# A two-layer decoder trunk on one core: seven block products for eight in half of an output projection, with changed orders around it

## The chip, the cores and the metric

The kernel runs on one core of a Trainium2 chip. Its time is the device time of one execution in microseconds. TensorE (PE) multiplies matrices, VectorE (DVE) and ScalarE (ACT) work element by element, GpSimd (POOL) and SyncE (SP) start transfers here. The kernel before has a median of 2151.49 us over three runs (2151.22 to 2151.53).

## The reference, cut to what matters

The trunk has 256 positions of 2048 features in float32. Layer 0 runs two recurrent mixers side by side, RG-LRU on 1024 features and HGRN2 on 1024, joins them and maps them by one output projection; layer 1 is an attention with its own output projection. Each layer ends in a squared-ReLU MLP of width 8192. The change touches the gates of the RG-LRU and the two output projections.

```python
def rg_lru(xb, w_a, b_a, w_i, b_i, lam):
    ...
    r = jax.nn.sigmoid(jnp.einsum('bshi,hij->bshj', xh, w_a.astype(F32)).reshape(bsz, seq, LRU_WIDTH)
                       + b_a.astype(F32))
    i = jax.nn.sigmoid(jnp.einsum('bshi,hij->bshj', xh, w_i.astype(F32)).reshape(bsz, seq, LRU_WIDTH)
                       + b_i.astype(F32))
    log_a = -LRU_C * r * jax.nn.softplus(-lam.astype(F32))
    ...

def recurrent_mixers(h, w_in, conv_w, conv_b, w_a, b_a, w_i, b_i, lam, lower_bound, g_norm, w_out):
    proj = h @ w_in
    x_lru, y_lru, q_h, f_h, v_h, g_h = jnp.split(proj, list(IN_SPLITS), axis=-1)
    lru = rg_lru(causal_depthwise_conv(x_lru, conv_w, conv_b), w_a, b_a, w_i, b_i, lam)
    lru = lru * jax.nn.gelu(y_lru.astype(F32), approximate=True)
    hg = hgrn2(q_h, f_h, v_h, g_h, lower_bound, g_norm)
    mixed = jnp.concatenate([lru, hg], axis=-1).astype(h.dtype)
    return mixed @ w_out
```

The residual is added to the result, and layer 0's MLP follows with its norm. In layer 1 the joined heads of the attention go through `w_o` in the same way.

## The kernel before, in words

**Numbers.** A float32 value is kept as a high and a low part. A product of two such values is three matmuls: high by high, high by low, low by high. Weights arrive as units of 128 x 2048 (1 MB, on SP's queue); ACT casts a unit to its high part (line 116, `hi`) and DVE subtracts to get the low part (line 117, `lo`). `bufa` and `bufb` hold a stage's input features as 16 blocks of 128 features, with the high half at columns 0 to 255 and the low half behind it.

**The order on each engine** is fixed when the program is built: a scheduler places the instructions by priority (`urgent`, `stream`) and by the order in which they are written, and `chain` strings all matmuls of line 210 in the written order. `units` is the written order of all weight units. `unit` hands out the next one and lets `fetch` load the one two places behind it.

**The recurrent stage** walks through units in the order of a string: x units give the conv's inputs, y units the gate branch, h units the heads of HGRN2, g units the gates. `lru_gates(gp)` (line 549) does four blocks of features, each with two gates `gr` and `gi`: a gate is two blocks by three matmuls of 256 columns, with a PSUM tile `p` of its own, and ACT's sigmoid (line 241 by its helper `lut`) reads it. The next weight unit is given to a list `late` there, and its cast is bound to come after the third gate's sigmoid (`gates[3:4]`, through `behind`). Pieces of HGRN2 (`po`, `pl`, `pt`, lines 484 to 527) and the recurrence (`z`, `q`, lines 584 to 588) lie between and beside these matmuls.

**An output projection** (`out_project`) runs over four groups of 512 columns. For one group, `tokens` takes two PSUM tiles, one per half of the rows (`j`), and four weight units `g`, each with four feature blocks. With `by_k`, as in the first group, the loop goes over feature blocks and takes both row halves for each; otherwise it finishes one half first. Layer 0's order of units is `kgs` = (2, 3, 0, 1), so that HGRN2's features, which are units 2 and 3, come first. `add_res` (line 629) adds to the residual, and `to_features` turns the new residual into the MLP's input and, for the first two groups, makes the linear combinations `formx` that the next paragraph needs (lines 612 to 618).

**Seven products for eight.** `blocks` multiplies two halves of the rows by two column groups over half of the feature blocks as a 2 x 2 block product with seven block products instead of eight (a, t1, t2, t3, t4, c, d); the other half of the features is done plainly (`n`). The combinations on the weight side are sums of whole units: `combine` makes them with DVE adds (line 148, `s`) and with loads that add onto a unit in memory on POOL's queue (`t`, `s`). The combinations on the input side are `formx` and `formh`. In before, `first` (over `w1`), `second` (over `w2`) and the q/k/v projection use it. `ORDERS` are the orders of its units; two of them differ in which of the plain units n 6 and n 7 comes first.

**Attention's end** (around line 932): for each head two matmuls into `po`, then ACT's cast into `bufb` (line 268), which layer 1's projection reads.

Of the kernel before, what the change touches and what calls it, by code (L numbers as in the profile page):

```python
# [10 lines left out]
F32 = mybir.dt.float32  # L11
# [4 lines left out]
AF = mybir.ActivationFunctionType  # L16
OP = mybir.AluOpType
# [3 lines left out]
P = 128  # L21
S = 256
D = 2048
KB = D // P
# [17 lines left out]
def trunk_kernel(ctx, tc, head, x, xtok, cols, tab, masks, pos, fin, w_in, w_gate, w_out, w_qkv, w_o, w1, w2, out):  # L42
# [27 lines left out]
    units = []  # L70
# [5 lines left out]

    order_of = lambda src, i: ORDERS[0 if src is w1 else 2 if src is w2 and i == 120 else 1]

# [6 lines left out]
    for step in ORDER.split():  # L85
        src, first, n = where[step[0]]
        units.extend((src, first(int(step[1])) + i) for i in range(n))
    units.extend((w_out, 4 * n + g) for n in range(4) for g in (2, 3, 0, 1))
    for layer in range(2):
# [11 lines left out]
    class Weights:  # L101
        def __init__(self, raw, step=2048, behind=()):
            self.raw = raw
            self.hi = whi.tile([P, 2048], F32R, name="hi")
            self.lo = wlo.tile([P, 2048], F32R, name="lo")
            self.behind = list(behind)
            for at in range(0, 2048, step) if step else ():
                self.split(at, step)

        def split(self, at, n, w=None):  # L110
            h, l = self.part(at, n)
            if w is None:
                w = self.raw[:, at:at + n]
            else:
                h, l = (t.rearrange("p (k c) -> p k c", c=512) for t in (h, l))
            casts[:] = [after(A.copy(h, w), self.behind)]  # L116
            i = V.tensor_tensor(l, w, h.bitcast(F32), OP.subtract)  # L117
            self.ins = getattr(i, "ins", i)
# [3 lines left out]

    def fetch(late=None):
        u = at[0]
        if u >= len(units):
            return
        at[0] += 1
        src, i = units[u][:2]
        with stream():
            if len(units[u]) > 2:  # L130
                combine(u, *units[u])
                return
            r = wraw.tile([P, 2048], F32, name="raw")
            loads[:] = [after(nc.sync.dma_start(r, src[i]), [])]
            if late is not None:
                late.append((u, r))
                return
            made[u] = Weights(r, 1024)
# [59 lines left out]

    def unit(src, i, late=None):
        u = at[1]  # L200
        assert units[u][0] is src and units[u][1] in (None, i), (u, i)
        at[1] += 1
        if u + 2 >= at[0]:
            fetch(late)
        return made.pop(u)
# [3 lines left out]
    def mm(*args, **kw):  # L209
        chain[:] = [after(T.matmul(*args, **kw), chain)]  # L210
# [123 lines left out]

    def tokens(src, i0, mov, kgs=(0, 1, 2, 3), by_k=False):
        ks = range(KB)
        ps = [pmm.tile([P, 512], F32, name="p") for _ in range(2)]
        for g in kgs:
            w = unit(src, i0 + g)
            order = [(j, i) for i in range(4) for j in range(2)] if by_k else \  # L340
                [(j, i) for j in range(2) for i in range(4)]
            for j, i in order:
                k = ks[4 * g + i]
                h, l = w.part(i * 512, 512)
                xh = mov[:, k, j * P:j * P + P]
                xl = mov[:, k, S + j * P:S + j * P + P]
                first, last = g == kgs[0] and i == 0, g == kgs[-1] and i == 3
                mm(ps[j], xh, h, start=first, stop=False)
                mm(ps[j], xh, l, start=False, stop=False)
                mm(ps[j], xl, h, start=False, stop=last)  # L350
            turn_some(1)
        return ps

# [195 lines left out]
    def lru_gates(gp):  # L549
        late, gates = [], []  # L550
        w = unit(w_gate, gp, late)
        gr = wk.tile([P, 4, S], F32, name="gr", bufs=1)
        gi = wk.tile([P, 4, S], F32, name="gi", bufs=1)
        for m in range(4):
            b = 4 * gp + m
            for gate, (g, bname) in enumerate(((gr, "b_a"), (gi, "b_i"))):
                p = pmm.tile([P, 512], F32, name="p")
                direct(p, w, [(gate * 8 + 2 * m + k, bufb[:, (b // 2) * 2 + k], k == 0, k == 1)
                              for k in range(2)])
                with urgent():  # L560
                    lut(g[:, m], p[:, :S], AF.Sigmoid, bias=col(bname, b))
                    gates.append(luts["now"][-1])
        with stream():
            for u, r in late:
                made[u] = Weights(r, 1024, gates[3:4])
        for m in range(4):
# [87 lines left out]

    def out_project(src, gname, kgs):
        nrm = Norm()
        for n in range(4):
            add_res(tokens(src, 4 * n, bufb, kgs, by_k=not n), n, nrm)
            to_features(n, gname, formx if n < 2 else None)
        return nrm  # L660

    nrm = out_project(w_out, "nmlp0", (2, 3, 0, 1))

# [115 lines left out]

    def second(i0, n0, nrm, r2, r2n, done, gains):  # L780
        def to_x(bank, j, n, r, last):
            at = slice(n * 512, n * 512 + 512)
            with urgent():
                read[:] = [after(V.scalar_tensor_tensor(xres[:, j, at], bank, r[:, j:j + 1], xres[:, j, at],
                                                        op0=OP.mult, op1=OP.add), [])]
                if nrm and last:
                    nrm.add(j, n, 0, S if ending and (j, n) == (1, LAST) else 512)
# [19 lines left out]
        def u3(bank):  # L807
            to_x(bank, 1, n0 + 1, r2n, True)
            done(n0 + 1)

        blocks(w2, i0, n0, bufb, formh,
               {"a": lambda b: to_x(b, 0, n0, r2, False), "t1": lambda b: to_x(b, 1, n0 + 1, r2, False),
# [4 lines left out]
    def mlp(layer, nrm, nxt, gname):  # L817
# [35 lines left out]
        return fing  # L853

    nx1 = Norm()
    mlp(0, nrm, nx1, "nmix1")
# [72 lines left out]
    def mix(hd, st, vg, bank="po", bufs=1):  # L929
        vs = slice((hd % 8) * P, (hd % 8) * P + P)  # L930
        po = psc.tile([P, S], F32, name=bank, bufs=bufs)
        T.matmul(po, vg[:, 0, vs], st[:, :S], start=True, stop=False, skip_group_check=True)  # L932
        T.matmul(po[:, P:], vg[:, 1, vs], st[:, S:], start=False, stop=True, skip_group_check=True)
        split_to(bufb[:, hd], po)
# [3 lines left out]

    lastv = []

# [48 lines left out]
    pair, formh = open_pairs(1)  # L989
    nrm = out_project(w_o, "nmlp1", (0, 1, 2, 3))  # L990
    fnorm = Norm(False)
# [82 lines left out]
def _layout(a):  # L1074
# [25 lines left out]
    def gate(w):  # L1100
# [19 lines left out]
        "fin": c(n(a["final_norm"]).reshape(1, D)),  # L1120
        "w_in": c(np.concatenate(w_in)), "w_gate": c(w_gate), "w_out": c(toks(n(a["rec_w_out"][0]))),
        "w_qkv": c(np.concatenate(w_qkv)), "w_o": c(toks(n(a["attn_w_o"][0]))),
# [20 lines left out]
```

## Time and profile before

| | |
|---|---|
| median of three runs | 2151.49 us (2151.22 to 2151.53) |
| profiled execution | 2151.35 us |
| its span | 2149.5 us |
| mean granted TensorE clock | 0.999 |
| data read from HBM | 481.76 MB, 225 GB/s over the span |
| cast of whole raw units on ACT (line 116) | 462 of 1494 ns mean |
| low part of them on DVE (line 117) | 462 of 1771 ns mean |

The profile is one execution, 1.85 us longer in device time than its span from the first to the last instruction. Terms of a sum that are worked out from the trace stand against this execution. A timeline row gives the start, the duration, the engine, the source line, the operation with its output and inputs, and in brackets the idle time before it and what ended that. Durations of matmuls overlap: the distance between starts says what one costs.

### The profile page before, as it was taken

The page shows a single profiled execution, that of the slowest core. Times are in us where ns is not written, and L with a number is a line of the kernel's source. Part 1 is how long each engine was busy: PE and PEld are TensorE (multiplying, and loading weights), DVE is VectorE, ACT ScalarE, POOL GpSimd, SP SyncE. Part 2 cuts the span into 40 slices and gives each one's busy share as a digit, 9 for nine tenths or more (in the row PEclk, how much of TensorE's full clock was granted, in tenths as well). Part 3 has the DMA queues.
Part 4 walks back from the last instruction along what each step waited for, and adds up shares of the span by engine and source line. Part 5 has one row for each costly group of instructions (what it writes and reads, how often), then busy time and mean ns, then how long its engine had stood idle before and what let it go on. Part 6 is the DMA issues. An engine that isn't in the chain of part 4 may idle for free.

```text
span 2149.5 us, 27705 instructions
## 1 busy us (share of the span) xinstructions
PE 2136.2 (99%) x11018; PEld 1830.3 (85%) x11018; DVE 1786.9 (83%) x2087; ACT 1267.6 (59%) x1407; POOL 61.8 (3%) x77
## 2 busy tenths in 40 slices
PE   9999999999999999999999999999999999999998
PEld 8999998888888888888888888888888888888887
DVE  7776787788888888889988897867988988888897
ACT  7444485566466566557665545456655755755764
POOL 0000000000000000000000000000000000000000
PEclk9999999999999999999999999999999999999999
DMA  8544445588878888887785556457878788787885
GB/s 323 175 157 157 154 149 209 179 240 268 249 240 263 257 243 243 277 245 234 240 268 198 173 160 232 157 185 226 237 240 283 240 240 260 262 241 243 272 261 156
DMA packets 68160, 485.64 MB, mean 226 GB/s; under 512 B 7600, under 2 KB 7856, under 8 KB 10048
## 3 DMA queue, kind: packets, MB, share of 16 engines
q1 hardware_dynamic: 57600, 410.89, 52.0%
q0 software_dynamic: 10144, 72.39, 18.3%
q8 instruction: 86, 1.41, 0.3%
q10 hardware_dynamic: 288, 0.61, 0.1%
q14 instruction: 42, 0.34, 0.0%
HBM read 481.76 MB, written 2.10 MB: 225 GB/s over the span
## 4 chain that ended last, share of the span: by engine, by line
PE 96%; ACT 2%; DVE 1%; DMA 0%; issue 0%; SPq 0%
PE p L210 66%; PE pd L210 13%; PE po L210 12%; PE pl L213 2%; PE pl L489 1%; PE pt L210 1%; DVE lo L117 1%; ACT hi L116 1%; DMA both_in<-in_head 0%; PE pl L911 0%; ACT gi L241 0%; ACT L241 0%; PE po L932 0%; PE pd L924 0%; ACT gr L241 0%; DVE xc L577 0%
## 5 line engine op out<-in xcount | busy, mean ns | idle before, releaser
L116 ACT CAST hi<-raw 128x2048 fp32r<-128x2048 f32 (+1 forms) x462 | 679.1, 1494 | 564.2 <-PE p L210 343.0
L117 DVE TENSOR_TENSOR lo<-raw,hi 128x2048 fp32r<-128x2048 f32 (+1 forms) x462 | 810.9, 1771 | 206.2 <-ACT hi L116 190.9
L210 PE MATMUL p<-hi,bufb 128*128 128x512 f32 x1408 | 449.0, 391 | 1.5 <-DVE z L438 1.1
L210 PE MATMUL p<-bufa,hi 128*128 128x256 f32 (+1 forms) x1792 | 367.2, 317 | 0.1
L210 PE MATMUL p<-hi,bufa 128*128 128x512 f32 x1136 | 363.3, 390 | 0.7 <-ACT bufa L271 0.7
L210 PEld LDWEIGHTS p<-hi,bufb 128*128 128x128 f32 x1408 | 264.3, 188 | 56.8 <-DVE z L438 1.5
L210 PEld LDWEIGHTS p<-bufa,hi 128*128 128x128 f32 x1792 | 294.9, 190 | 18.6 <-DVE hz L438 0.3
L210 PE MATMUL p<-lo,bufb 128*128 128x512 f32 x704 | 274.2, 390 | 0.0
L210 PE MATMUL p<-bufa,lo 128*128 128x256 f32 x1152 | 256.2, 287 | 0.0
L210 PEld LDWEIGHTS p<-hi,bufa 128*128 128x128 f32 x1136 | 213.1, 188 | 45.0 <-ACT bufa L271 0.9
L117 DVE TENSOR_TENSOR lo<-s,hi 128x2048 fp32r<-128x2048 f32 x102 | 233.1, 2285 | 14.5 <-ACT hi L116 12.3
L116 ACT CAST hi<-s 128x2048 fp32r<-128x2048 f32 x102 | 195.1, 1913 | 51.7 <-PE po L210 22.2
L210 PE MATMUL p<-lo,bufa 128*128 128x512 f32 x568 | 221.4, 390 | 0.2 <-DVE lo L117 0.2
L210 PEld LDWEIGHTS p<-bufa,lo 128*128 128x128 f32 x1152 | 189.7, 191 | 2.7
L210 PEld LDWEIGHTS p<-lo,bufb 128*128 128x128 f32 x704 | 132.2, 188 | 26.9
L210 PEld LDWEIGHTS p<-lo,bufa 128*128 128x128 f32 x568 | 106.6, 188 | 22.6 <-DVE lo L117 0.6
L210 PE MATMUL pd<-hi,bufa 128*128 128x512 f32 x288 | 95.2, 392 | 0.0
L210 PE MATMUL p<-hi,formx 128*128 128x512 f32 x288 | 94.8, 390 | 0.0
L117 DVE TENSOR_TENSOR lo<-t,hi 128x2048 fp32r<-128x2048 f32 x34 | 77.8, 2288 | 13.0 <-ACT hi L116 13.0
L210 PE MATMUL po<-hi,bufa 128*128 128x512 f32 x256 | 84.9, 393 | 0.0
L210 PE MATMUL p<-hi,formh 128*128 128x512 f32 x256 | 84.0, 389 | 0.0
L210 PE MATMUL pd<-hi,bufb 128*128 128x512 f32 x256 | 83.0, 389 | 0.0
(307 smaller groups left out, 2892.0 us busy)
## 6 DMA issues: line engine op xcount, KB each, us to landing
raw<-in_w SPq DMA_DIRECT2D x224, 1024.0 KB, 6.5
raw<-in_w_qkv SPq DMA_DIRECT2D x46, 1024.0 KB, 4.9
raw<-in_w_in SPq DMA_DIRECT2D x45, 1024.0 KB, 4.9
t<-in_w SPq DMA_DIRECT2D x32, 1024.0 KB, 6.4
t<-in_w POOLq DMA_DIRECT2D x32, 1024.0 KB, 8.9
s<-in_w POOLq DMA_DIRECT2D x32, 1024.0 KB, 9.3
raw<-in_w_out SPq DMA_DIRECT2D x16, 1024.0 KB, 4.9
raw<-in_w_o SPq DMA_DIRECT2D x16, 1024.0 KB, 4.8
```

The source lines that it names most:

```text
L116: casts[:] = [after(A.copy(h, w), self.behind)]
L117: i = V.tensor_tensor(l, w, h.bitcast(F32), OP.subtract)
L210: chain[:] = [after(T.matmul(*args, **kw), chain)]
L213: chain[:] = [after(T.transpose(out_, in_, ident), chain)]
L489: T.matmul(pl[:, j], kq[:, js], halves(qp[:, js], c, True), start=True, stop=True)
```

## The change

Layer 0's output projection does its third and fourth column groups by `second`, that is by `blocks` with seven products for eight over feature blocks 0 to 7, and plainly over 8 to 15. `mixed_forms` makes the combinations of the projection's input out of `bufb` for four pairs of feature blocks, written behind certain weight units of the first two groups. The weights of `w_out` are stored in the order `PAIRED`, and `tokens` follows it. `by_k` stays for layer 1's first group alone. The factors of the residual add are then the plain numbers 1.0 and -1.0.

Around it: `w1`'s first pair of column groups takes the order with n 7 before n 6. The two gates of a block share one PSUM tile, each with its half, and the list `late` with the hold on the cast is gone. In layer 1's first projection group, the second feature block of the last unit is chained behind the last `po` matmul of the attention (`lastpo`). The call for layer 0's projection stands after the definition of `mlp`, since `second` has to be defined first.

```diff
-    order_of = lambda src, i: ORDERS[0 if src is w1 else 2 if src is w2 and i == 120 else 1]
+    order_of = lambda src, i: ORDERS[0 if src is w1 and i not in (0, ) else 2 if src is w2 and i == 120 else 1]
...
-    units.extend((w_out, 4 * n + g) for n in range(4) for g in (2, 3, 0, 1))
+    units.extend((w_out, 4 * n + g) for n in range(2) for g in (2, 3, 0, 1))
+    plan2(w_out, 8)
...
-            casts[:] = [after(A.copy(h, w), self.behind)]
+            casts[:] = [after(A.copy(h, w), [])]
...
-    def tokens(src, i0, mov, kgs=(0, 1, 2, 3), by_k=False):
-        ks = range(KB)
+    def tokens(src, i0, mov, kgs=(0, 1, 2, 3), by_k=False, behind=(), then=()):
+        ks = PAIRED if any(src is w for w in (w_out, )) else range(KB)
...
                 first, last = g == kgs[0] and i == 0, g == kgs[-1] and i == 3
+                if g == kgs[-1] and (i, j) == (1, 0):
+                    chain.extend(behind)
...
             turn_some(1)
+            for m in then[kgs.index(g)] if then else ():
+                mixed_forms(m)
...
     def lru_gates(gp):
-        late, gates = [], []
-        w = unit(w_gate, gp, late)
+        w = unit(w_gate, gp)
...
             b = 4 * gp + m
+            p = pmm.tile([P, 512], F32, name="p")
             for gate, (g, bname) in enumerate(((gr, "b_a"), (gi, "b_i"))):
-                p = pmm.tile([P, 512], F32, name="p")
-                direct(p, w, [(gate * 8 + 2 * m + k, bufb[:, (b // 2) * 2 + k], k == 0, k == 1)
+                q = p[:, gate * S:gate * S + S]
+                direct(q, w, [(gate * 8 + 2 * m + k, bufb[:, (b // 2) * 2 + k], k == 0, k == 1)
                               for k in range(2)])
                 with urgent():
-                    lut(g[:, m], p[:, :S], AF.Sigmoid, bias=col(bname, b))
-                    gates.append(luts["now"][-1])
-        with stream():
-            for u, r in late:
-                made[u] = Weights(r, 1024, gates[3:4])
+                    lut(g[:, m], q, AF.Sigmoid, bias=col(bname, b))
...
-    def out_project(src, gname, kgs):
+    def mixed_forms(m):
+        z = pair.tile([P, 2, 2, P], F32, name="y1", bufs=2)
+        b = bufb[:, 2 * m:2 * m + 2].bitcast(F32)
+        V.tensor_tensor(z.rearrange("p i j c -> p i (j c)"), b[..., :S], b[..., S:], OP.add)
+        a11, a21, a12, a22 = (z[:, i, j] for i in range(2) for j in range(2))
+        combos(a22, a11, a21, a12, a11, a21, a12, a22)
+        part_forms(formh, m, 1, slice(0, 4), z.rearrange("p i j (one c) -> p one (i j) c", one=1))
+
+    def out_project(src, gname, kgs, behind=()):
         nrm = Norm()
-        for n in range(4):
-            add_res(tokens(src, 4 * n, bufb, kgs, by_k=not n), n, nrm)
+        whole = any(src is w for w in (w_out, ))
+        for n in range(2 if whole else 4):
+            then = () if not whole else ((((), (0,), (1,), (2,)), ((), (), (3,), ())) if src is w_out else
+                                         (((), (), (), (0, 1)), ((), (2,), (3,), ())))[n]
+            add_res(tokens(src, 4 * n, bufb, kgs, src is w_o and not n, () if n else behind, then), n, nrm)
             to_features(n, gname, formx if n < 2 else None)
+        if whole:
+            second(0, 2, nrm, 1.0, -1.0, lambda n: to_features(n, gname, None), None, src)
         return nrm
...
-    def second(i0, n0, nrm, r2, r2n, done, gains):
+    def second(i0, n0, nrm, r2, r2n, done, gains, src=w2):
...
+                r = r if isinstance(r, float) else r[:, j:j + 1]
...
-        blocks(w2, i0, n0, bufb, formh,
+        blocks(src, i0, n0, bufb, formh,
...
-        T.matmul(po[:, P:], vg[:, 1, vs], st[:, S:], start=False, stop=True, skip_group_check=True)
+        lastpo[:] = [after(T.matmul(po[:, P:], vg[:, 1, vs], st[:, S:], start=False, stop=True, skip_group_check=True), [])]
...
-    nrm = out_project(w_o, "nmlp1", (0, 1, 2, 3))
+    nrm = out_project(w_o, "nmlp1", (0, 1, 2, 3), lastpo)
...
-        "w_in": c(np.concatenate(w_in)), "w_gate": c(w_gate), "w_out": c(toks(n(a["rec_w_out"][0]))),
+        "w_in": c(np.concatenate(w_in)), "w_gate": c(w_gate), "w_out": c(toks(n(a["rec_w_out"][0]), PAIRED)),
```

Left out are the removed parameters of `Weights`, `fetch` and `unit` that carried the hold, and the move of the call.

More of the change, by code (lines that the diff above doesn't have):

```diff
@@ L101, in trunk_kernel, with __init__ @@
     class Weights:
-        def __init__(self, raw, step=2048, behind=()):
+        def __init__(self, raw, step=2048):
             self.raw = raw
@@ L105, in __init__ @@
             self.lo = wlo.tile([P, 2048], F32R, name="lo")
-            self.behind = list(behind)
             for at in range(0, 2048, step) if step else ():
@@ L121, in part, with fetch @@
             return self.hi[:, at:at + n], self.lo[:, at:at + n]
-    def fetch(late=None):
+    def fetch():
         u = at[0]
@@ L134, in fetch @@
             loads[:] = [after(nc.sync.dma_start(r, src[i]), [])]
-            if late is not None:
-                late.append((u, r))
-                return
             made[u] = Weights(r, 1024)
@@ L197, in fetch_first, with unit @@
                 made[u].split(1024 * m, 1024)
-    def unit(src, i, late=None):
+    def unit(src, i):
         u = at[1]
@@ L203, in unit @@
         if u + 2 >= at[0]:
-            fetch(late)
+            fetch()
         return made.pop(u)
@@ L653, in to_features @@
         turns.extend([-half if forms else 0, lambda half=half: work(half)] for half in range(2))
-    def out_project(src, gname, kgs):
-        nrm = Norm()
-        for n in range(4):
-            add_res(tokens(src, 4 * n, bufb, kgs, by_k=not n), n, nrm)
+    def mixed_forms(m):
[6 more added lines that the diff above has]
+    def out_project(src, gname, kgs, behind=()):
+        nrm = Norm()
+        whole = any(src is w for w in (w_out, ))
[3 more added lines that the diff above has]
+            add_res(tokens(src, 4 * n, bufb, kgs, src is w_o and not n, () if n else behind, then), n, nrm)
             to_features(n, gname, formx if n < 2 else None)
+        if whole:
+            second(0, 2, nrm, 1.0, -1.0, lambda n: to_features(n, gname, None), None, src)
         return nrm
-    nrm = out_project(w_out, "nmlp0", (2, 3, 0, 1))
     def blocks(src, i0, n0, mov, forms, events, final):
@@ L783, in to_x @@
             with urgent():
-                read[:] = [after(V.scalar_tensor_tensor(xres[:, j, at], bank, r[:, j:j + 1], xres[:, j, at],
+                r = r if isinstance(r, float) else r[:, j:j + 1]
+                read[:] = [after(V.scalar_tensor_tensor(xres[:, j, at], bank, r, xres[:, j, at],
                                                         op0=OP.mult, op1=OP.add), [])]
@@ L853, in mlp @@
         return fing
+    nrm = out_project(w_out, "nmlp0", (2, 3, 0, 1))
     nx1 = Norm()
@@ L937, in trunk_kernel @@
         rt = rstd(nx1)
-    lastv = []
+    lastv, lastpo = [], []
     def values(i0):
```

## The prediction

> **What bounds the kernel now.** I read the first page for the busy shares and the chain of waits, then the view of TensorE's (PE's) waits, then windows and timelines of the three stages that the change touches: the recurrent gates, layer 0's output projection, layer 1's output projection.
>
> ```profile
> span 2149.5 us, 27705 instructions
> PE 2136.2 (99%) x11018; PEld 1830.3 (85%) x11018; DVE 1786.9 (83%) x2087; ACT 1267.6 (59%) x1407; POOL 61.8 (3%) x77
> PE 96%; ACT 2%; DVE 1%; DMA 0%; issue 0%; SPq 0%
> ```
>
> PE is busy for 2136.2 of 2149.5 us and is 96% of the chain that ended last. So only two things change the time by much: the number of matmul columns, and gaps on PE. Gaps are few now:
>
> ```profile
> PE p L210 <- DVE z L438: 1.4, 2, 1.1
> ...
> PE p L210 <- ACT gr L241: 0.9, 1, 0.9
> ...
> PE p L210 <- ACT bufb L268: 0.5, 1, 0.5
> ```
>
> They total under 3 us; each one that vanishes or appears counts in full, because nothing else can make up for it on a full PE. The stages, by windows (us, then busy time of PE, PEld, DVE, ACT, POOL, granted clock, DMA share, GB/s):
>
> ```profile
> 268.22:275.77 7.55, 7.55 (x66) 7.55 (x65) 6.45 (x20) 6.13 (x15) 0.00 (x0) 1.00 0.13 51
> 301.60:309.11 7.51, 6.26 (x50) 5.85 (x49) 7.36 (x25) 6.74 (x17) 0.00 (x0) 1.00 0.35 136
> 334.30:420.00 85.70, 85.70 (x390) 71.00 (x391) 56.84 (x74) 46.61 (x69) 1.00 (x1) 1.00 0.64 213
> 450.00:1100.00 650.00, 650.00 (x2946) 539.62 (x2945) 570.32 (x413) 406.42 (x339) 27.31 (x32) 1.00 0.81 250
> ```
>
> The first two are the two groups of recurrent gates. ACT and DVE are close to full in them, which in no other row here is so for both: what the change does to ACT's order there is paid by PE. The third is the output projection of layer 0, with room on DVE; the fourth, layer 0's MLP in the seven-product form, shows that PE stays full with DVE at 570.32/650 = 88%.
>
> **The change, part by part.**
>
> *Seven products for eight.* A block product is four blocks of features by three matmuls of 512 columns. The second pair of column groups loses one: 12 matmuls.
>
> ```profile
> 336.00 0.39 PE L210 MATMUL p<-lo,bufb 128*128 128x512 f32 x1
> ...
> 338.72 0.39 PE L210 MATMUL p<-lo,bufb 128*128 128x512 f32 x1
> ```
>
> From one lo matmul to the fourth after it are 12 matmuls: 338.72 - 336.00 = 2.72 us. **Term 1: -2.72.**
>
> What it adds must hide under PE. On DVE these are four sets of combinations of the mixer's output (one add and one lo of 512 columns, four adds of 128 each), three more lo halves of whole weight units, and two sums of weight units:
>
> ```profile
> L117 DVE TENSOR_TENSOR lo<-raw,hi 128x1024 fp32r<-128x1024 f32 x28 | 33.1, 1222 | 18.6 <-ACT hi L116 18.5
> ...
> L612 DVE TENSOR_TENSOR formx<-y,formx 128x512 fp32r<-128x512 f32 x4 | 2.7, 685 | 0.0
> L148 DVE TENSOR_TENSOR s<-raw,t 128x2048 f32<-128x2048 f32 x1 | 2.3, 2293 | 0.6 <-DMA raw<-in_w 0.6
> ...
> L615 DVE TENSOR_TENSOR y<-y 128x128 f32<-128x128 f32 x4 | 1.2, 292 | 0.1
> ```
>
> A set is 2 x 0.685 + 4 x 0.292 = 2.54 us, four are 10.2. The second pair's weights go from 8 units in two halves (16 x 1.222 = 19.6) to 11 lo and 2 sums of 2.29 (29.8): +10.2. DVE's 56.84 becomes about 77 in 85.70 - 2.72 = 83 us, or 93%: above the 88% of the MLP. Following DVE, ACT and the loads unit by unit with these durations I find no matmul waiting; the tightest is the lo of the last plain unit, about 1.1 us before PE wants it. SyncE issues as many loads as before. POOL's queue gets two more, which add a second unit onto one already loaded:
>
> ```profile
> t<-in_w POOLq DMA_DIRECT2D x32, 1024.0 KB, 8.9
> ```
>
> With 8.9 us to landing they are there some 8 us before their cast, and nothing else stands on POOL's queue at that time. I take nothing for all this, and keep 0 to +3.5 us (two lo and more late, less what the margin pays). That the MLP's first quarter takes its two plain column groups in the other order, since the projection's two groups now end in the other order, moves no work: the group that it starts with is the one that is ready.
>
> *The first matmul of the projection's second half.* Now the first group goes over rows within each block of features, and its second PSUM tile is wanted after three matmuls, while DVE still reads it:
>
> ```profile
> 332.83 0.39 PE L210 MATMUL p<-hi,bufb 128*128 128x512 f32 x1
> 334.27 0.50 PE L210 MATMUL p<-hi,bufb 128*128 128x512 f32 x1 [1.05 <-DVE z L438]
> ```
>
> The new order finishes 12 matmuls on one tile first, so the second is wanted nine matmuls (9 x 2.72/12 = 2.0 us) later: longer than the gap. Slot to slot, PE starts 334.27 - 332.83 = 1.44 later against 0.23 for one matmul, and the matmul after the wait takes 0.11 longer: **term 2: -1.3.** Late next would be nothing: the MLP's own weights are loaded by the same rule.
>
> *Layer 1's projection.* The attention's last mixing matmuls (`po`) go 12 matmuls earlier into the first group, so that ACT's cast is done in time.
>
> ```profile
> 1402.93 0.50 PE L210 MATMUL p<-hi,bufb 128*128 128x512 f32 x1 [0.46 <-ACT bufb L268]
> ```
>
> The 2.72 us gained cover 0.46 and the 0.1 of restart: **term 3: -0.56.**
>
> *The gates.* This is the part that costs. Each of four features' blocks needs two gates of six 256-column matmuls. Now the gates have a PSUM tile each, and the cast of the next weight unit is held on ACT until after the third gate. After, both gates share a tile, and the program makes the second gate's first matmul wait until ACT has read the first; the hold is gone, and the cast stands ahead of the first gate's activation in ACT's queue. First group, PE then ACT:
>
> ```profile
> 268.22 0.40 PE L210 MATMUL p<-bufb,hi 128*128 128x256 f32 x2
> ...
> 268.58 0.40 PE L210 MATMUL p<-bufb,hi 128*128 128x256 f32 x2
> ...
> 269.30 0.39 PE L514 MATMUL po<-vg,st 128*128 128x128 f32 x2
> ...
> 269.67 0.48 PE L210 MATMUL p<-bufb,hi 128*128 128x256 f32 x2
> ...
> 270.11 0.56 PE L489 MATMUL pl<-qk 128*128 128x64 f32 x4
> 270.47 0.48 PE L210 MATMUL p<-bufb,hi 128*128 128x256 f32 x2
> ...
> 275.77 0.40 PE L210 MATMUL p<-bufa,hi 128*128 128x256 f32 x2
> ```
> ```profile
> 268.88 0.61 ACT L543 ACTIVATE xc<-xp,c__88 128x256 f32<-128x256 f32 x1 [1.83 <-DVE xp L438]
> 269.39 0.46 ACT L241 ACTIVATE gr<-p,c__88 128x256 f32<-128x256 f32 x1
> ...
> 272.55 1.99 ACT L116 CAST hi<-raw 128x1024 fp32r<-128x1024 f32 x2
> ```
>
> A gate is 6 x 0.12 = 0.72 (268.22 to 268.58 is three). PE is at the second gate at 268.22 + 0.72 + 0.37 (po, 269.30 to 269.67) + 0.36 (pl, 270.11 to 270.47) = 269.67. ACT starts the casts, whose buffer PE frees at 268.22, at 268.3: 1.89 by start, then xc 0.51, then gr 0.46, to 271.16; PE 0.06 later. A wait of 1.55. The second pair waits an estimated 0.39 for DVE's qk, which I place by DVE's order of now; the third and fourth each from the last matmul's slot 0.20 to ACT's start + 0.47 + 0.06, less 0.36 of pl that now stands there: 0.37 each. With four restarts of 0.1, and 48 matmuls (5.76), po and five pl (1.8): 0.37 + 5.76 + 1.8 + 2.68 + 0.4 = 11.0, against 7.55. Two pl (0.72, and 0.16 of their restarts) come out of the units behind: **term 4: 3.45 - 0.9 = +2.5.**
>
> Second group, which begins 2.5 later, at 304.1:
>
> ```profile
> 301.60 0.40 PE L210 MATMUL p<-bufb,hi 128*128 128x256 f32 x2
> ...
> 303.56 0.50 PE L210 MATMUL p<-bufb,hi 128*128 128x256 f32 x2 [0.36 <-DVE z L438]
> ...
> 308.30 0.50 PE L210 MATMUL p<-bufb,hi 128*128 128x256 f32 x2 [0.89 <-ACT gr L241]
> ...
> 309.11 0.40 PE L210 MATMUL p<-bufa,hi 128*128 128x256 f32 x2
> ```
> ```profile
> 302.60 0.42 ACT L241 ACTIVATE q<-q 128x256 f32<-128x256 f32 x1 [0.20 <-DVE q L585]
> ...
> 308.78 0.65 ACT L524 ACTIVATE ho<-po,hr 128x128 f32<-128x128 f32 x2
> ```
>
> ACT's order there becomes q, half a cast, two ho, the other half, then gr. From q's end at 303.02 + 2.5 = 305.5: 1.0 + 0.65 + 1.0 + 0.46 gives 308.6 for PE. It was ready at 304.1 + 0.72 + 0.23 (the transpose of ho, now between the gates) = 305.0: a wait of 3.6, cut in two by the transpose, which itself waits for ho at 307.1. The next three pairs have no cover: one waits 1.03 behind ACT's q and bufb, two 0.73. Sum: 5.76 + 0.23 + 3.6 + 2.5 + 0.4 = 12.5, against 309.11 - 301.60 = 7.5, less the 0.23 that leaves the unit behind: **term 5: +4.7.** Everything behind ACT's gr here is recurrent work of the next group, which PE feeds later too.
>
> As to whether that wait is needed, the row is the window 301.60 to 309.11: with two tiles PE lost 7.51 - 5.76 = 1.75 us for all reasons. [...] Before has no shared tile to test it on.
>
> **Sum:** -2.72 - 1.3 - 0.56 + 2.5 + 4.7 = +2.6. On the profiled execution's 2151.35 us that is 2154.0; the runs' median 2151.49 is 0.14 above it, so **2154.2 us.**
>
> **The rivals.**
>
> *A, faster: the gate waits are covered.* If gr of the first gate is read while PE still has other work, terms 4 and 5 go, and so do the 1.75 that the second group loses now: 2151.5 - 2.72 - 1.3 - 0.56 - 1.75 = 2145.2. For it: only gaps of 0.36 and 0.89 show now, ACT being 59% busy in all. Against it: ACT is busy for 6.74 of 7.51 us there, and nothing stands between the gates of three pairs. With half of the waits covered it is 2149 to 2151.
>
> *B, slower: DVE becomes the bound of the projection's second pair.* At 93%, DVE slips by more than its 1.1 us at the last plain unit. It decides from there: each lo behind is late by as much. Two lo late are 4.6 - 1.1 = 3.5: up to 2157.7. For it: the 93%; against: the MLP at 88% shows no gap at all.
>
> *C, slower: the clock falls in the long wait.* After PE's last work the records show:
>
> ```profile
> 2143.00:2146.00 3.00, 0.00 (x0) 0.00 (x0) 1.43 (x4) 1.33 (x2) 0.00 (x0) 1.00 0.37 152
> 2146.00:2149.50 3.50, 0.00 (x0) 0.00 (x0) 0.00 (x0) 0.00 (x0) 0.00 (x0) 0.50 0.42 170
> ```
>
> Over 3 us idle kept 1.00, then came 0.50. A wait of 3.6 reaches that, if the two transposes inside don't count as work; 3.5 us at half rate cost 1.75, two such stretches 3.5: 2155.9 to 2157.7. [...]
>
> *D: the change doesn't save its twelve matmuls* because the combined weights of the pair come late by one product: 2154.2 + 2.72 = 2156.9. Against: loads of this kind keep up in the MLP.
>
> **How the numbers follow.** Chances: forecast 0.50 (2152.6 to 2155.7, the two gate terms by a quarter either way), A whole 0.09, A half 0.06, B 0.20, C 0.10, D 0.05. A measurement here can tell 0.2%, or 4.3 us: faster is below 2147.2, slower above 2155.8. Faster: A whole, 0.09. Same: the forecast and half of A, 0.56. Slower: B, C, D, 0.35. The range leaves out A whole and the top of B and C: 2149.5 to 2158.2.
>
> **What would show it.** Terms 4 and 5: new rows of PE waiting for gr in the view of waits, some 2.3 us in the first group and 6 in the second, the longest split by two transposes at about 307. Term 1: 12 fewer matmuls, and the projection 2.7 shorter. Terms 2 and 3: the rows with z (1.05) and bufb (0.46) gone. B: PE waiting for lo or s between 375 and 425. C: granted clock below 1.00 between 305 and 320. I am wrong if the gate groups take under 9 us each, or if PE waits in the projection.

## The result, and the profile after

| | before | after |
|---|---|---|
| median | 2151.48 us, ten runs (2150.96 to 2152.62) | 2159.18 us, ten runs (2155.13 to 2160.53) |
| ratio | | 1.003, 95% interval 1.002 to 1.0039 |
| profiled execution, its span | 2151.35, 2149.5 | 2159.37, 2157.6 |

The change makes the kernel slower, by 7.7 us at the median. The ten runs of the changed kernel lie on two levels: four between 2155.13 and 2155.76 and six between 2159.15 and 2160.53; those of before lie within 1.7 us of each other. The profiled execution is one of the upper level. First the page and the view of PE's waits of the changed kernel:

```profile
span 2157.6 us, 27722 instructions
PE 2139.4 (99%) x11006; PEld 1833.1 (85%) x11006; DVE 1806.3 (84%) x2112; ACT 1275.7 (59%) x1406; POOL 63.6 (3%) x79
```
```profile
PE p L207 <- ACT gr L238: 4.3, 7, 1.3
PE pt L528 <- ACT ho L525: 2.2, 1, 2.2
...
PE p L207 <- ACT bufa L268: 0.5, 1, 0.5
```

PE does 12 matmuls fewer (11006 for 11018), yet is busy 3.2 us longer. So part of the loss is not waiting: matmuls themselves became slower. The waits are the seven for `gr` and the one in front of the transposes `pt`; those for `z` and `bufb` are gone. PE's timeline of the changed kernel, at the borders of the stages:

```profile
268.16 0.40 PE L207 MATMUL p<-bufb,hi 128*128 128x256 f32 x2
...
271.14 0.50 PE L207 MATMUL p<-bufb,hi 128*128 128x256 f32 x2 [1.26 <-ACT gr L238]
...
279.19 0.40 PE L207 MATMUL p<-bufa,hi 128*128 128x256 f32 x2
...
303.72 0.40 PE L207 MATMUL p<-bufb,hi 128*128 128x256 f32 x2
...
306.82 0.59 PE L528 MATMUL pt<-tab__180,ho 128*128 128x128 f32 x2 [2.22 <-ACT ho L525]
308.38 0.50 PE L207 MATMUL p<-bufb,hi 128*128 128x256 f32 x2 [0.98 <-ACT gr L238]
...
313.04 0.63 PE L207 MATMUL p<-bufb,hi 128*128 128x256 f32 x2
313.47 0.41 PE L207 MATMUL p<-bufb,lo 128*128 128x256 f32 x1
314.45 0.80 PE L207 MATMUL p<-bufb,hi 128*128 128x256 f32 x2 [0.56 <-ACT gr L238]
...
319.39 0.63 PE L207 MATMUL p<-bufa,hi 128*128 128x256 f32 x2
...
344.09 0.40 PE L207 MATMUL p<-hi,bufb 128*128 128x512 f32 x1
...
431.24 0.39 PE L207 MATMUL pd<-hi,bufa 128*128 128x512 f32 x1
```

The first group of gates takes 279.19 - 268.16 = 11.03 us, against 7.55. The second starts at 303.72, waits 2.22 and 0.98 behind ACT, and then its matmuls get slow: two and one of them take 0.63 + 0.41 where they took 0.40 + 0.28. It ends at 319.39, 15.67 us after its start, against 7.51. The windows say why (us, busy time of PE, PEld, DVE, ACT, POOL, granted clock, DMA share, GB/s; the last two are short ones at the borders):

```profile
304.00:309.50 5.50, 2.30 (x16) 1.79 (x16) 5.47 (x14) 4.91 (x11) 0.00 (x0) 1.00 0.55 191
309.50:323.00 13.50, 11.81 (x52) 10.93 (x52) 5.58 (x12) 7.11 (x15) 0.00 (x0) 0.50 0.23 79
323.00:326.00 3.00, 3.00 (x27) 3.00 (x26) 0.80 (x4) 2.99 (x5) 0.00 (x0) 0.96 0.70 221
309.50:309.75 0.25, 0.25 (x3) 0.25 (x3) 0.25 (x2) 0.09 (x1) 0.00 (x0) 0.63 0.00 0
323.00:323.50 0.50, 0.50 (x6) 0.50 (x5) 0.50 (x3) 0.50 (x1) 0.00 (x0) 0.78 0.00 0
```

TensorE's granted clock goes from full to half. A mean of 0.63 over 0.25 us puts its fall at 309.56, and 0.78 over 0.50 us puts its return at 323.22. So it is at half for 13.7 us, 3.8 us of which fall into the unit behind the gates. The projection, from its first matmul to the MLP's first combined product, takes 431.24 - 344.09 = 87.15 us. In before it was 423.62 - 332.36 = 91.26:

```profile
332.36 0.40 PE L210 MATMUL p<-hi,bufb 128*128 128x512 f32 x1
...
423.62 0.39 PE L210 MATMUL pd<-hi,bufa 128*128 128x512 f32 x1
```

From the first gate's first matmul to the start of PE's last, the changed kernel takes 2147.59 - 268.16 = 1879.43 us and before 2140.70 - 268.22 = 1872.48. These 6.95 us are the change's. The other 1.1 of the spans' difference lies almost wholly behind PE's last matmul, where the last write of the output takes 4.4 us to land for 3.2. Among the fourteen profiles of this study five have 4.1 to 4.4 there and the other nine about a microsecond less; what decides it stays open. The last rows of PE of the two kernels (after, then before):

```profile
2147.59 0.28 PE L207 MATMUL pt<-hi,bufb 128*128 128x256 f32 x1
```
```profile
2140.70 0.28 PE L210 MATMUL pt<-hi,bufb 128*128 128x256 f32 x1
```

### The profile page after: what moved, and what is told of

Same layout as the page of the kernel before. It is cut to its first block, busy times and chain, and to the rows that moved or that the text cites. A ratio compares the mean times of both kernels' runs of the same rounds, so it can differ in the third digit from the quotient of the medians.

```text
span 2157.6 us, 27722 instructions
## 1 busy us (share of the span) xinstructions
PE 2139.4 (99%) x11006; PEld 1833.1 (85%) x11006; DVE 1806.3 (84%) x2112; ACT 1275.7 (59%) x1406; POOL 63.6 (3%) x79
## 4 chain that ended last, share of the span: by engine, by line
PE 97%; DVE 1%; ACT 1%; DMA 0%; issue 0%; SPq 0%; ACTq 0%
PE p L207 66%; PE pd L207 13%; PE po L207 13%; PE pl L210 2%; PE pl L490 1%; PE pt L207 1%; DVE lo L117 0%; DMA x_in<-in_x 0%; PE pl L922 0%; PE po L943 0%; PE pd L935 0%; ACT hi L116 0%; ACT gr L238 0%; PE pd L474 0%; PE pl L921 0%
## 5 line engine op out<-in xcount | busy, mean ns | idle before, releaser
L207 PE MATMUL p<-hi,bufb 128*128 128x512 f32 x1336 | 426.7, 391 | 0.0
L207 PEld LDWEIGHTS p<-hi,bufb 128*128 128x128 f32 x1336 | 250.8, 188 | 51.9
L207 PE MATMUL p<-lo,bufb 128*128 128x512 f32 x668 | 260.2, 389 | 0.0
L117 DVE TENSOR_TENSOR lo<-s,hi 128x2048 fp32r<-128x2048 f32 x105 | 239.9, 2285 | 12.5 <-ACT hi L116 10.3
L116 ACT CAST hi<-s 128x2048 fp32r<-128x2048 f32 x105 | 201.0, 1914 | 50.7 <-PE po L207 22.4
L207 PEld LDWEIGHTS p<-lo,bufb 128*128 128x128 f32 x668 | 125.5, 188 | 25.5
L207 PE MATMUL po<-hi,bufb 128*128 128x512 f32 (+1 forms) x288 | 92.0, 386 | 0.0
L207 PE MATMUL p<-hi,formh 128*128 128x512 f32 x272 | 89.3, 389 | 0.0
```

The source lines that it names most:

```text
L116: casts[:] = [after(A.copy(h, w), [])]
```

## The experiments

Twelve runs follow: eleven edited kernels, and the changed kernel once more. A kernel's median stands beside the median of before on the same chips, which was 2151.36 to 2151.51 us throughout.

**Both parts of the gates undone.** The changed kernel with a tile for each gate and with the hold. The hold binds the cast to `gates[3:4]`, which is the fourth sigmoid of the group; the texts ahead call it the third.

```diff
-            p = pmm.tile([P, 512], F32, name="p")
             for gate, (g, bname) in enumerate(((gr, "b_a"), (gi, "b_i"))):
-                q = p[:, gate * S:gate * S + S]
+                p = pmm.tile([P, 512], F32, name="p")
+                q = p[:, :S]
...
+        with stream():
+            for u, r in late:
+                made[u] = Weights(r, 1024, gates[3:4])
```

> The changed kernel with the gates of before: a PSUM tile for each gate, and the next unit's cast held until after the fourth gate's activation. Theory (all of the loss is in the gates): PE's waits for gr go back to 0.36 and 0.89 in the second group, the granted clock stays 1.00 between 300 and 330, and what is left is the gain of the two projections, 2151.49 - 4.1 - 0.6 = 2146.8 us (2146.3 to 2147.5), below both kernels, with no second level near 2159. Rival (the second pair of column groups, not the gates, makes DVE late): the time stays above 2153.

Measured: 2146.80 us (2146.15 to 2147.97, 11 runs), ratio 0.9979 (0.997 to 0.9988). The waits in the gates are those of before, and the clock is 1.00. The whole loss, and the second level, is in the gates; the projections gain what the terms said. The runs spread over 1.8 us, and at least part of that is the start of the program: in this profile the first group of gates begins at 269.38, in the next at 267.89, before anything that was edited.

**Two tiles, no hold.** The first half of that diff alone.

> The changed kernel with a PSUM tile for each gate again, but without the hold: the cast stays ahead of the first gate's activation on ACT. Three PSUM buffers let PE run three gates before it must wait for the first activation. Theory: nothing extra in the first group, about 2.2 us of waiting in the second (activation read at 306.1 in before's times, PE there at 303.9), against 1.75 lost in before: 2147 to 2148.8 us. Rival (the order of the cast alone makes the loss, the tile is innocent): 2155 or more, with a wait of 3 us and over and a clock that falls.

Measured: 2145.93 us (2145.46 to 2147.19, 8 runs), ratio 0.9975 (0.9965 to 0.9985), the fastest kernel of the study. Its second group in PE's timeline:

```profile
301.07 0.40 PE L207 MATMUL p<-bufb,hi 128*128 128x256 f32 x2
...
302.94 0.51 PE L207 MATMUL p<-bufb,hi 128*128 128x256 f32 x2 [0.27 <-DVE z L439]
...
304.64 0.50 PE L207 MATMUL p<-bufb,hi 128*128 128x256 f32 x2 [0.72 <-ACT gr L238]
...
308.33 0.40 PE L207 MATMUL p<-bufa,hi 128*128 128x256 f32 x2
```

It takes 7.26 us, no longer than before's 7.51. So the order of the cast was not the cause by itself, and the rival falls: undoing the shared tile alone takes away the whole loss. The time is 1.1 us below my range, for I expected 2.2 us of waiting here and there are 0.99. The two casts do stand ahead of `gr` in ACT's timeline, but they start at 301.93, and the two `ho` that stood between them come after the gates:

```profile
301.93 1.98 ACT L116 CAST hi<-raw 128x1024 fp32r<-128x1024 f32 x2
...
304.13 0.46 ACT L238 ACTIVATE gr<-p,c__88 128x256 f32<-128x256 f32 x1
...
311.14 0.62 ACT L525 ACTIVATE ho<-po,hr 128x128 f32<-128x128 f32 x2
```

PE has three gates to work on meanwhile, and waits at the fourth, 0.72 us at 304.64.

**The hold back, one tile.** The second half of the diff alone.

> The changed kernel with the hold on the cast again, but with both gates in one tile. Theory: the wait behind the first activation is short (0.3 to 0.8), but the casts then stand ahead of the third pair's activation, so PE waits about 1.5 to 2 us there, and 0.4 to 0.7 at the other pairs: some 2 us in the first group and 2.7 over before in the second; no wait reaches 3 us, so the clock stays 1.00: 2150.5 to 2152.5 us, one level only. Rival (the removed hold alone makes the loss): as the kernel with both restored, 2146.8. Rival (the shared tile alone makes the loss): 2155 or more.

Measured: 2154.39 us (2153.19 to 2156.33, 10 runs), ratio 1.0015 (1.0006 to 1.0024). The longest row of PE in its second group:

```profile
313.21 0.51 PE L211 MATMUL p<-bufb,hi 128*128 128x256 f32 x2 [2.41 <-ACT gr L242]
```

The place was right, the third pair behind the casts; the wait was 2.41 for the 1.5 to 2, and the sum 2 us over my range. The rival of the hold falls. That of the tile misses its 2155 at the median, but comes nearest: with one tile the group takes 12.45 us with the hold, and 12.25 and 12.47 without it in the two profiles below in which the clock is kept. What the hold takes away is the long fall of the clock, which none of the ten runs has by its time. The clock is 1.00 in this profile. The four runs above 2155.6 are in no profile; their mean clock on record, 0.997 to 0.998 against 0.998 to 0.999 of the others, leaves room for a short fall.

**Before with nothing but the changed gates.**

> The kernel before with nothing but the changed gates: one tile for both, no hold. Theory: the loss of the changed kernel without its gains: 2151.49 + 4.0 + 4.75 = 2160.2 where the clock holds and 2151.49 + 8.0 + 4.75 = 2164.2 where it falls to half for some 13 us after the wait in the second group, so two levels 4 us apart among the runs. Rival (the changed gates cost something only together with the new projection): 2151.5 to 2153.

Measured: 2161.73 us, five runs at 2156.41, 2156.63, 2161.73, 2162.92 and 2163.16; ratio 1.004 (1.0028 to 1.0053). The two levels are there without any of the new projection. All five are 1 to 4 us lower than expected. The row of 1.05 for `z` is not in this kernel's view of waits either, and its projection takes 89.89 us for 91.26: with PE later out of the gates, DVE is in time. So the gates' loss and term 2's gain don't add. Of the 3.6 us missing at the lower level that is 1.4; another 1.2 is a short fall of the clock that the changed kernel's lower level has (below) and this profile has not, and 0.9 is the last write of the output, 3.2 us here for 4.1 there. The profile is the run of 2156.63, and its timeline and windows show something else:

```profile
306.62 0.58 PE L527 MATMUL pt<-tab__180,ho 128*128 128x128 f32 x2 [2.23 <-ACT ho L524]
308.18 0.51 PE L210 MATMUL p<-bufb,hi 128*128 128x256 f32 x2 [0.98 <-ACT gr L241]
```
```profile
303.50:309.50 6.00, 2.79 (x21) 2.28 (x20) 5.96 (x16) 4.96 (x12) 0.00 (x0) 1.00 0.49 175
309.50:316.00 6.50, 4.59 (x35) 3.99 (x34) 2.87 (x8) 3.41 (x8) 0.00 (x0) 1.00 0.50 161
```

PE waits 2.23 and 0.98 us around the transposes, as in the changed kernel, and the clock stays at 1.00. The second group takes 12.47 us. So these two waits alone do not always make the clock fall.

**Term 2 alone.** In before:

```diff
-            add_res(tokens(src, 4 * n, bufb, kgs, by_k=not n), n, nrm)
+            add_res(tokens(src, 4 * n, bufb, kgs, by_k=not n and src is w_o), n, nrm)
```

> The kernel before with one edit: the first column group of layer 0's projection finishes one half of the rows first, instead of both halves block by block. Theory (term 2): the wait of 1.05 for z goes, nothing takes its place: 2151.45 - 1.3 = 2150.1 us. Rival (a wait for z or for another reader of the same buffers comes nine matmuls later): 2151 to 2151.5, with the row of 1.05 moved or split.

Measured: 2150.08 us (2149.8 to 2150.94, 11 runs), ratio 0.9992 (0.9983 to 1.0001). The median moved by 1.28, as expected, and the projection takes 89.92 us for 91.26; the interval of the ratio just touches 1.

**Term 2 taken out of the fastest kernel.** Two tiles, no hold, and the first group done block by block for both halves:

> The kernel with two tiles and no hold, with the first column group of layer 0's projection again done block by block for both halves of the rows: the seven products without the other order. Theory (term 1 alone in the projection): the wait of about 1.05 for z is back, 2145.9 + 1.3 = 2147.2 us, and from the projection's first matmul to the MLP's first combined product 87.2 + 1.3 = 88.5 us. Rival (the seven products need the other order, or their combinations come late): another wait there, 2148 or more.

Measured: 2146.18 us (2145.92 to 2147.16, 9 runs). The wait did not come back:

```profile
332.79 0.40 PE L207 MATMUL p<-hi,bufb 128*128 128x512 f32 x1
...
333.26 0.78 PE L207 MATMUL p<-hi,bufb 128*128 128x512 f32 x2
...
420.14 0.39 PE L207 MATMUL pd<-hi,bufa 128*128 128x512 f32 x1
```

The projection takes 87.35 us, 0.2 more than with the new order. Here DVE reads that `z` 0.28 us after the projection's first matmul, for 1.44 in before. The other order is worth 1.3 us in before and next to nothing in this kernel; the seven products don't need it.

**Term 3.** Two tiles, no hold, and the call without `lastpo`:

```diff
-    nrm = out_project(w_o, "nmlp1", (0, 1, 2, 3), lastpo)
+    nrm = out_project(w_o, "nmlp1", (0, 1, 2, 3))
```

> The kernel with two tiles and no hold, without the chaining behind the last mixing matmuls in layer 1's projection. Theory (term 3): the wait of 0.46 for bufb comes back: 2145.9 + 0.6 = 2146.5 us. Rival (the wait was already gone for another reason): 2145.9.

Measured: 2147.09 us (2146.54 to 2148.19, 11 runs), 1.2 above the kernel with it, for an expected 0.6. The row of 0.5 for `bufb` is back in its view of waits. From the MLP's first combined product to PE's last matmul, which leaves the varying start out, it takes 1717.09 us for 1716.29, 0.8 longer. The kernel of term 2 alone, which has before's order of `w1`'s units and no `lastpo` either, takes the same 1717.09; so that changed order costs nothing there.

**The wait filled.** The changed kernel with matmuls that nobody reads:

```diff
                     lut(g[:, m], q, AF.Sigmoid, bias=col(bname, b))
+                if gp == 1 and m == 0 and gate == 0:
+                    idle = pmm.tile([P, 512], F32, name="p")
+                    for _ in range(3):
+                        direct(idle, w, [(k, bufb[:, (b // 2) * 2 + k], k == 0, k == 1) for k in range(2)])
```

> The changed kernel with 18 more matmuls of 256 columns (2.16 us), whose result nobody reads, between the first and the second gate of the second group, where PE waits 2.22 and 0.98 us. The ends on ACT are not moved. Theory (the idleness of PE makes the clock fall): PE now waits less than 1 us at a time there, the clock stays 1.00, and all runs lie at the lower level, 2155.0 to 2156.0 us, though there is more work. Rival (the clock falls for another reason, such as the load of the other engines): two levels as before, 2155.3 and 2159.3, or 2157.5 and 2161.5 if the work is not covered.

Measured: 2154.10 us (2153.82 to 2155.67, 11 runs), ratio 1.0013 (1.0005 to 1.0022): below even the lower level of the changed kernel, with 18 matmuls more. PE's timeline and its windows:

```profile
303.50 0.40 PE L207 MATMUL p<-bufb,hi 128*128 128x256 f32 x2
...
308.17 0.51 PE L207 MATMUL p<-bufb,hi 128*128 128x256 f32 x2 [0.98 <-ACT gr L238]
...
310.43 0.50 PE L207 MATMUL p<-bufb,hi 128*128 128x256 f32 x2 [0.56 <-ACT gr L238]
...
315.75 0.40 PE L207 MATMUL p<-bufa,hi 128*128 128x256 f32 x2
```
```profile
303.50:308.10 4.60, 3.62 (x28) 3.12 (x26) 4.40 (x13) 3.99 (x9) 0.00 (x0) 1.00 0.71 228
308.10:316.00 7.90, 6.13 (x45) 5.53 (x46) 4.61 (x11) 4.42 (x13) 0.00 (x0) 1.00 0.41 135
```

The waits behind `gr` are the same, the clock stays 1.00, and the group takes 12.25 us. That shows the long fall of this kernel's clock to come from PE's idleness in that wait. Three of the eleven runs are above 2155.3; none falls for long.

**The wait filled by a third.** The same with `range(1)`, six matmuls:

> The changed kernel with only 6 matmuls of 256 columns (0.72 us) between the first and second gate of the second group, so that PE still idles about 1.5 and 1.0 us there, against 2.2 and 1.0 in the changed kernel. Theory (idleness within a few us decides, and where a run stands against it is chance): some runs still fall, fewer than the 6 of 10 of the changed kernel, at 2158 and over; the others at 2154 to 2155.7. If one wait of 2 us and over is what counts, no run falls. Rival (only whether anything runs counts): as many fall as in the changed kernel.

Measured, seven runs: 2153.95, 2155.12, 2155.43, 2156.21, 2159.17, 2160.18 and 2160.33. Three of seven still fall for long by their times and their mean clocks on record (0.995 to 0.996, for 0.998 to 0.999 of the other four), and the profile, which is the run of 2159.17, shows the clock at half from 309.5 to 323 (0.53 over 309.5 to 310.0, 0.82 over 323.0 to 323.5). So no single wait of 2 us is needed, for this kernel's waits there are 1.5 and 0.98:

```profile
306.87 0.59 PE L528 MATMUL pt<-tab__180,ho 128*128 128x128 f32 x2 [1.51 <-ACT ho L525]
308.43 0.51 PE L207 MATMUL p<-bufb,hi 128*128 128x256 f32 x2 [0.98 <-ACT gr L238]
```

That fewer fall than in the changed kernel can't be told from seven runs.

**The changed kernel again.**

> The changed kernel once more, on this chip beside the others: two levels again, near 2155.3 and 2159.3, both with the same waits of PE in the gates, the upper one alone with the clock at half between about 310 and 323. Rival (the upper level belonged to one chip or one load): one level.

Measured: one run at 2155.57 and four at 2159.64 to 2160.65. This time the profile is of the lower level, and it shows that I was wrong about that level (windows, then PE's timeline):

```profile
304.00:308.50 4.50, 1.44 (x10) 0.93 (x8) 4.47 (x14) 3.91 (x9) 0.00 (x0) 0.99 0.65 233
308.50:312.00 3.50, 2.93 (x12) 2.63 (x12) 3.10 (x7) 2.27 (x8) 0.00 (x0) 0.52 0.41 98
312.00:316.00 4.00, 3.29 (x24) 2.98 (x24) 0.93 (x3) 1.80 (x5) 0.00 (x0) 1.00 0.42 176
```
```profile
303.98 0.40 PE L207 MATMUL p<-bufb,hi 128*128 128x256 f32 x2
...
317.47 0.40 PE L207 MATMUL p<-bufa,hi 128*128 128x256 f32 x2
```

The clock falls here too, for 3.4 us instead of 13.7 (a mean of 0.95 over 308.0 to 308.5 puts the fall at 308.45, and 0.63 over 311.5 to 312.0 the return at 311.87), and the group takes 13.49 us: 1.24 more than with the filled wait, and 2.18 less than the 15.67 of the upper level. The upper level loses another 344.09 - 319.39 - (340.51 - 317.47) = 1.7 between the second group and the projection, whose first matmul starts at 340.51 here.

**The shared tile in the first group alone.**

> The changed kernel with the shared tile kept in the first group of gates alone; the second group has a tile for each gate; no hold in either. Theory: term 4 alone is left over the kernel with two tiles, 2145.9 + 2.5 = 2148.4 us (2147.9 to 2149.3), the longest wait is 1.3 us and the clock stays 1.00: no level 4 us above. Rival (the first group's waits are part of what makes the clock fall): a second level near 2152.

Measured: 2150.23 us (2149.91 to 2152.18, 11 runs), ratio 0.9996 (0.9987 to 1.0005); seven runs up to 2150.70 and four from 2151.54. The clock is 1.00 throughout in its profile, and no run is 4 us above. But it costs 4.3, not 2.5. PE's timeline shows where the rest is:

```profile
304.22 0.40 PE L207 MATMUL p<-bufb,hi 128*128 128x256 f32 x2
...
306.92 0.50 PE L207 MATMUL p<-bufb,hi 128*128 128x256 f32 x2 [1.10 <-DVE z L439]
```

The second group, with two tiles, now waits 1.10 for `z` instead of 0.27: the first group's delay moves DVE's work into it, and the group takes 8.37 us for 7.26. Another 0.9 is the last write of the output, which takes 4.2 us here and 3.2 in the kernel with two tiles. What sets the four upper runs apart stays open, since none of them is in a profile.

**The combinations made twice**, in the fastest kernel, to measure the room on DVE:

```diff
                 mixed_forms(m)
+                mixed_forms(m)
```

> The kernel with two tiles and no hold, with each set of combinations of the projection's input made twice: 10.2 us more on DVE (4 x 2.54) inside the first two column groups. DVE is busy for 79.8 of 87 us in the projection's window there, so 90 of 87 would be wanted. Theory (DVE's slack in the projection is real but small): part of it fits, and PE waits for lo, 1 to 6 us in all: 2147 to 2152 us. Rival (DVE has slack in the first two groups, which do not use the weight sums, and the tight second pair comes later): 2145.9, no wait.

Measured: 2154.67 us (2152.98 to 2155.17, 10 runs), ratio 1.0012 (1.0003 to 1.0021), 2.7 above my range. PE's timeline, and the windows before and behind that row:

```profile
387.75 0.79 PE L207 MATMUL p<-hi,formh 128*128 128x512 f32 x1 [5.91 <-ACT formh L609]
```
```profile
340.00:380.00 40.00, 40.00 (x182) 33.13 (x181) 39.10 (x68) 23.20 (x32) 1.00 (x1) 1.00 0.69 225
387.00:394.00 7.00, 6.25 (x17) 4.99 (x18) 5.25 (x4) 3.88 (x5) 0.86 (x1) 0.52 0.18 76
```

With 10.2 us more, DVE is full (39.10 of 40) and PE waits 5.9 for the last set of combinations, not for `lo`. The clock falls in this wait and is at half for 6.8 us (a mean of 0.89 over 386.5 to 387.0 puts the fall at 386.89, and 0.78 over 393.5 to 394.0 the return at 393.72), which brings the rest. By the estimate of 10.2 the room ahead of that row was thus 10.2 - 5.9 = 4.3 us.

## Why the prediction was right or wrong

The direction, the place and the waits of the forecast were right; the size was not. The forecast was 2154.2 and the median came out at 2159.18, 1.0 above the top of the range. The range was said to leave out the top of rival C, but it held all that C was priced at, up to 2157.7. The step that failed is the price of rival C, the fall of the clock: at most 3.5 us in the prediction, 5.1 in the profile of the upper level.

- **The sum.** Where the wait is filled and the clock holds, PE takes 2142.24 - 267.95 = 1874.29 us from the first gate to its last matmul, 1.8 more than before, for a forecast of 2.6. That this kernel's median (2154.10) is the forecast is in part chance: its last write too takes 4.2 us to land, 1.0 that no term foresaw.
- **Terms 4 and 5, the gates.** The first group was put at 11.0 us and took 11.03; it moved the second group's start by 303.72 - 301.60 = 2.1, for 2.5. The second was put at 12.5 and takes 12.25 where the clock holds (the filled wait). PE was put at 308.6 for the first `gr` and came at 308.38. Net of the 0.23 that leaves the unit behind, term 5 is 12.25 - 7.51 - 0.23 = 4.5, for 4.7. Both stand.
- **Rival A is refuted**, whole and half: the waits are there, row by row, and the kernel that differs in the tile alone does without the loss. Seven of the eight second gates wait for the reader of the first one's half, 0.17 to 1.26 us each, though the halves are disjoint. That shows what the program guards; whether the guard is needed was not shown, since no run here leaves it out.
- **Term 1.** Between the two kernels that both finish one half of the rows first, before's projection (89.92) and the one of the kernel without `lastpo` (419.05 - 331.88 = 87.17), it is 2.75, for 2.72.
- **Term 2.** -1.28 alone in before, for -1.3. But as a term of this sum it was counted where it doesn't stand alone: with changed gates the wait is gone anyway. The total stands all the same, since the new order and the later PE take away one and the same wait.
- **Term 3.** -0.8 to -1.2, for -0.56. The wait was priced by its row alone.
- **Rival B** did not happen: no row of PE waits for `lo`, `s` or `formh` in the projection. Its margin was given as 1.1 us at the last plain unit, which no run measured. The doubled combinations show 4.3 us of room further ahead, and the first thing late there is another one.
- **Rival C is what happened, in both profiles of the changed kernel**, and this is the step that failed. I gave it 0.10 with "3.5 us at half rate cost 1.75, two such stretches 3.5", since the two transposes might count as work. Against the filled wait, the fall costs 1.2 us at the lower level and 15.67 - 12.25 + 1.7 = 5.1 at the upper one. The upper price was missed because I let the clock come back after one or two stretches. It stayed at half for 13.7 us, through pairs of gates in which PE still waited 0.56 every 3.5 us, and came back at 323.22, 3.8 us into the dense work of the next unit. The falls measured here last 3.4 us at the lower level, 6.8 with the doubled combinations and 13.7 at the upper level (and in the profile with six matmuls more), that is one, two and four times the shortest; why was not shown.
- **What decides between the levels stays open.** The fall begins 1.2 us after PE's second wait ends in the profile of the upper level (309.56 and 308.38) and 0.2 us before that in the one of the lower level (308.45 and 308.65). So the fall comes at different times against the same waits, but that this alone sets the level was not shown. Before with the changed gates had the same two waits, which began 0.2 us earlier than at the upper level, and kept its clock.

## What to carry to other kernels

Of the eight pairs of gates that shared a PSUM tile here, seven made PE wait for ACT's read of the first gate, 4.3 us in all. A tile each cost nothing here, with three buffers, and undoing that one edit, the shared tile, turned 2159 us into 2145.9. A gap on PE has to be priced twice, once by its length and once by what the clock does after it: here its fall added 1.2 us in one profile and 5.1 in another, and did not come in a third with the same two waits. Where gaps stand close together, as 1.5 and 0.98 us did here, look at the granted clock in the windows behind them, and read the spread of the runs. Gains and losses of stages that follow each other don't add where both decide the same wait.

## What the runs showed of the hardware

The clock fell at waits of 2.22 and 0.98 us with two transposes between them, in both profiles of the changed kernel, and at 1.51 and 0.98 in the profile with six matmuls more, and for three of that kernel's seven runs by time and mean clock. The same waits, 2.23 and 0.98, left it at 1.00 in the profile of before with the changed gates. It did not fall in the profile with one wait of 0.98 and three of 0.56, and none of that kernel's eleven runs was near the upper level. With the clock at half, PE was busy for 11.81 of 13.50 us at the upper level and for 2.93 of 3.50 at the lower one, so its busy share was alike in the long fall and the short one; what brings the clock back stays open.
